# Three tiles for half rows of modulation weights, four for raw weights, and a later point at which a half row is taken

## The chip, the cores and the metric

The kernel runs on one core of a Trainium2 chip. The metric is device time in microseconds for one execution; a difference is judged on several executions of both kernels on the same chip. The core has a matmul engine (TensorE, PE), a vector engine (VectorE, DVE), a scalar engine (ScalarE, ACT), GpSimd (POOL) and SyncE (SP), which issues nearly all DMA transfers of this kernel. Each engine runs its own instructions in program order.

## The reference

A two-layer trunk on 256 tokens of width 2048, in float32. Each layer has a mixer and a SwiGLU FFN; each of the four sub-layers is normalised, modulated and gated by numbers made from one vector `c`:

```python
def ada_modulation(c, w, b):
    mod = (jax.nn.silu(c) @ w + b)[:, None, :]
    shift, scale, gate = jnp.split(mod, 3, axis=-1)
    return shift, scale, gate
...
    shift, scale, gate = ada_modulation(c, ada_mix_w[i], ada_mix_b[i])
    h = rms_norm(x) * (1.0 + scale) + shift
    ...
    x = x + gate * y
```

In layer 0 the mixer is RWKV-7 and a gated delta net side by side behind one input projection and one output projection; in layer 1 it is Mamba-2. The modulation weights are 4 sub-layers × 2048 × 6144 numbers, 201 MB: they are read once and used for one vector only.

## The kernel before

**Weights of the projections.** They come in pieces of up to 128 × 1024 float32 (512 KB), in the order in which they are used (`seq`, made by `plan`). Each is loaded into a *raw* tile (`rawt`, `RAW` of them, line 575). ACT copies it to a reduced-precision high part `whi` (`split_next`, line 697), DVE subtracts to get the low part `wlo` (`low_parts`, line 712), and PE multiplies high by high, high by low and low by high (`products`). A raw tile is free when its low part is made; `issue_raw` (line 594) then has SP load the next piece into it. Of `whi` and `wlo` there are `PARTS` = 3 each.

**Modulation weights.** PE isn't used for them. DVE takes one row of 2048 weights per output channel block: a multiply with silu(c) and a sum. The first 32 rows (shift and scale of the first sub-layer) come whole, 1 MB each, into `INI` = 6 tiles of their own, in `seq` among the first slab's pieces. All other 160 rows come in two halves of 512 KB each, into `adat` tiles (`ADAS` of them, line 587). `adaq` lists the 320 halves in order, each with a due time counted in pieces of `seq`. The functions:

- `issue_ada` (line 617) has SP load the next half into a free `adat` tile, if it is at most `EARLY` = 48 pieces ahead of its due time. While other halves are on the way it waits until the tile's last use lies behind the planned PE clock.
- `take_ada` (line 650) does one half on DVE (`ada_half`), which frees its tile, and calls `issue_ada`.
- `fill_ada` (line 638) decides whether a half is taken now. It is called after each step of `products`, and in `force`.
- `modc` (line 655) is called by whoever needs a shift, scale or gate. If the row isn't known it takes halves until it is, whatever `fill_ada` would say.

**The order of the work.** The program is written in one order by a planner, `Clock`. It keeps an estimated time for each engine (`clock.at`) and for each tile its last write or read (`clock.since`; for a tile that a DMA fills, the estimated landing). In the FFNs and the mixers PE's products set the pace, and everything else is slipped in between by these estimates: `run` steps the chains of the mixer, `prefetch` splits the next piece when DVE and ACT are less than `SOON` = 1000 ns ahead of PE, and `fill_ada` takes halves. Its rule: a half that is due may be taken while DVE's estimate is at most `LATE` = 2000 ns ahead of PE's, one that isn't due only while DVE is at least 500 ns behind (`FILL`).

**The slab.** A sub-layer's first matmuls (`lin_slab`, line 780) run over the 16 input tiles in the outer loop and 14 output tiles (8 in layer 1) inside, so that PE can start when the first input tile is ready. Three tiles ahead, `ahead` makes the input: `norm_mod` multiplies on DVE by the norm, `shifted` (line 838) adds the shift on ACT (`hhi`) and on DVE (`hlo`). The shift comes from `modc`.

**Names in the profile.** `adat` are the half rows (`adap` and `mod` the sums that they give), `ini` the whole rows, `raw` the raw tiles, `whi` and `wlo` the parts, `hhi` and `hlo` the parts of the input, `t` the normed input. All operations are recorded on line 373, where a helper issues them, so groups are told apart by tiles.

Of the kernel before, what the change touches and what calls it, by code (L numbers as in the profile page):

```python
# [85 lines left out]
LAG = 4  # L86
SOON = 1000.0
INI = 6
RAW = 5
PIECE = 8  # L90
LEAD = 2
PARTS = 3
WORK0 = 6
WORK1 = 10
IDLE = 500.0
ADAS = 2
FILL = -500.0
LATE = 2000.0
DUE = 1.0
# [297 lines left out]
def trunk(ctx: ExitStack, tc: tile.TileContext, I, out):  # L397
    nc = tc.nc
    clock = Clock()
# [11 lines left out]
    ET = mybir.EngineType  # L411
# [81 lines left out]
    def force(stop):  # L493

        while not stop():
            c = min((c for c in chains if not blocked(c)), key=lambda c: c.ready)
            fill_ada(c.ready - IDLE)
            step(c)
# [53 lines left out]
    def plan(w, adas):  # L552

        a = [r + (e,) for r in adas for e in range(2)]
        adaq.extend(r + (len(seq) + int(DUE * i * len(w) / len(a)),) for i, r in enumerate(a))
        seq.extend(w)
# [17 lines left out]
    plan(wf1[88:], [])  # L574
    rawt = [wp.tile([P, 1024], F32, name=f"raw{q}") for q in range(RAW)]
    rname = [name_of(t) for t in rawt]
    rfree = list(range(RAW))
    ini = ExitStack()
# [7 lines left out]
    after_ada = {}  # L586
    adat = [wp.tile([P, 1024], F32, name=f"adat{q}") for q in range(ADAS)]
    aname = [name_of(t) for t in adat]
# [28 lines left out]
    def issue_ada():  # L617
        while adaq and len(adas) < ADAS and adaq[0][4] <= st["item"] + EARLY:
            q = next(q for q in range(ADAS) if q not in [a[0] for a in adas])
            if adas and clock.since(aname[q]) > clock.at(ET.PE) + QUEUE:  # L620
                return
            adas.append((q,) + adaq.pop(0))
            load_ada(adat[q], *adas[-1][1:5])
# [14 lines left out]
    def fill_ada(until=None):  # L638

        issue_ada()  # L640
        while adas:
            q, l, r, n, e, due = adas[0]
            v = clock.at(ET.DVE)
            if until is None:
                until = clock.at(ET.PE) + (LATE if due <= st["item"] else FILL)
            if v > until or clock.since(aname[q]) > until:
                return
            take_ada()

    def take_ada():  # L650
        q = adas.pop(0)
        ada_half(adat[q[0]], *q[1:5])
        issue_ada()
# [100 lines left out]
    def products(units, hi, lo, o, act):  # L754

        ahi, alo = act
        n = len(units)
        lag = min(LAG, n)
        w = lambda t, i: t[:, (o + i) * P:(o + i + 1) * P]
        for i in range(n + lag):  # L760
            if i < n:
                ps, kt, a, z = units[i]
                PE.matmul(ps, w(hi, i), ahi[:, kt, :], start=a, stop=False)
                PE.matmul(ps, w(hi, i), alo[:, kt, :], start=False, stop=False)
            if i >= lag:
                ps, kt, a, z = units[i - lag]
                PE.matmul(ps, w(lo, i - lag), ahi[:, kt, :], start=False, stop=z)
            if i % STEP == STEP - 1 or i == n + lag - 1:
                low_parts()
                issue_raw()  # L770
                run()
                if max(clock.at(ET.DVE), clock.at(ET.Activation)) < clock.at(ET.PE) + SOON:
                    prefetch()
                fill_ada()
# [1216 lines left out]
```

## Time and profile before

| | |
|---|---|
| median of 3 runs | 3009.4 us (3009.3 to 3010.23) |
| the profiled execution | 3007.3 us, of which the span of its instructions is 3005.5 us |
| mean granted clock of PE | 0.985 |
| ACT, POOL busy | 1437.3 us, 166.0 us |
| moved by DMA | 706.30 MB, mean 235 GB/s |
| DVE on half rows | 160 × 1322 ns and 160 × 1302 ns |
| half rows: issue to landing | 4.8 us median, 3.2 to 11.6 us |
| raw pieces: issue to landing | 4.2 us median, 2.8 to 11.9 us |

Busy times are unions of an engine's instructions. In a view of waits each row says which instruction stood idle, what ended its wait, then the total in us, the number of times and the longest in us. In a timeline a row has the start in us from the start of the span, the duration in us, and in brackets the idle time before it with what ended it. A view of windows has one row per stretch: busy us of PE, of its weight loads, of DVE, ACT and POOL with their counts, PE's granted clock, the share of the DMA engines and GB/s; restricted to one tile's instructions it has only the engines that these use.

### The profile page before, as it was taken

Reading aid. Unit: us, or ns where it says so; the run is one execution under the profiler, and the core shown is the slowest. Engines: PE = TensorE matmul, PEld = TensorE weight load, DVE = VectorE, ACT = ScalarE, POOL = GpSimd, SP = SyncE. Lnnn points to the kernel's source line nnn. Section 1 sums busy time; section 2 is a strip of 40 time slices with the busy share of each in tenths; the row PEclk is TensorE's granted clock in tenths of the full one; section 3 lists DMA queues with packets and bytes.
Section 4 is the critical chain, followed back from the end, with each engine's and each line's share of the span. In section 5 each row is a group of like instructions: output and inputs, shape, how many; then the busy total and the mean of one; then the engine's idle time right before and its main releaser. Section 6 shows DMA issues by size and latency. Waiting matters only on the chain.

```text
span 3005.5 us, 61406 instructions
## 1 busy us (share of the span) xinstructions
PE 2876.6 (96%) x25098; PEld 2806.8 (93%) x25098; DVE 2198.9 (73%) x3442; ACT 1437.3 (48%) x2363; POOL 166.0 (6%) x191
## 2 busy tenths in 40 slices
PE   6789999997899999999999999999999999999998
PEld 6788889987799999999999999999999999999998
DVE  6987897888777787777778878888767754544555
ACT  3354555544344444444446566555445444444444
POOL 3400001000000000000000111111000000000000
PEclk9899999998999999999999999999999999999999
DMA  9865464576887898788866666666866755655554
GB/s 387 349 199 183 143 216 158 166 276 237 285 285 277 286 331 311 280 284 275 281 208 204 214 208 229 221 225 229 279 221 237 272 184 174 200 184 189 185 174 154
DMA packets 237307, 706.30 MB, mean 235 GB/s; under 512 B 36912, under 2 KB 55648, under 8 KB 236768
## 3 DMA queue, kind: packets, MB, share of 16 engines
q1 hardware_dynamic: 236448, 699.46, 68.4%
q8 instruction: 196, 3.21, 0.4%
q10 hardware_dynamic: 576, 2.92, 0.3%
q14 instruction: 87, 0.71, 0.1%
HBM read 695.70 MB, written 6.58 MB: 234 GB/s over the span
## 4 chain that ended last, share of the span: by engine, by line
issue 52%; PE 21%; DVE 2%; ACT 1%; POOL 0%; DMA 0%; DVEq 0%; POOLq 0%; ACTq 0%
PE bank L373 21%; ACT whi L373 1%; DVE wlo L373 0%; DVE hlo L373 0%; DVE t0b L373 0%; DVE adat L373 0%; DVE x L373 0%; DVE w L373 0%; POOL mgsa L373 0%; DVE ymix L373 0%; DMA adat<-in_ada 0%; DVE mar L373 0%; ACT t L373 0%; DVE mxs L373 0%; DVE sqacc L373 0%
## 5 line engine op out<-in xcount | busy, mean ns | idle before, releaser
L373 PE MATMUL bank<-hhi,whi 128*128 128x256 f32 x5568 | 1472.6, 286 | 38.2 <-ACT whi L373 36.0
L373 PE MATMUL bank<-hlo,whi 128*128 128x256 f32 x5568 | 1450.4, 282 | 3.3 <-DVE hlo L373 2.9
L373 DVE TENSOR_TENSOR wlo<-raw,whi 128x1024 fp32r<-128x1024 f32 (+3 forms) x1005 | 1112.0, 1121 | 422.8 <-ACT whi L373 418.9
L373 ACT ACTIVATE whi<-raw 128x1024 fp32r<-128x1024 f32 (+3 forms) x1005 | 966.5, 971 | 691.5 <-PE bank L373 653.3
L373 PE MATMUL bank<-hhi,wlo 128*128 128x256 f32 x5568 | 1121.8, 284 | 26.2 <-DVE wlo L373 26.0
L373 PEld LDWEIGHTS bank<-hhi,whi 128*128 128x128 f32 x5568 | 1061.0, 191 | 56.5 <-ACT whi L373 42.9
L373 PEld LDWEIGHTS bank<-hlo,whi 128*128 128x128 f32 x5568 | 1061.4, 191 | 6.5 <-DVE hlo L373 4.6
L373 PEld LDWEIGHTS bank<-hhi,wlo 128*128 128x128 f32 x5568 | 858.4, 190 | 37.4 <-DVE wlo L373 31.8
L373 PE MATMUL bank<-glo,whi 128*128 128x256 f32 x1408 | 351.1, 281 | 0.0
L373 PE MATMUL bank<-ghi,whi 128*128 128x256 f32 x1408 | 351.1, 281 | 0.0
L373 PEld LDWEIGHTS bank<-glo,whi 128*128 128x128 f32 x1408 | 265.0, 188 | 0.0
L373 PEld LDWEIGHTS bank<-ghi,whi 128*128 128x128 f32 x1408 | 265.0, 188 | 0.0
L373 PE MATMUL bank<-ghi,wlo 128*128 128x256 f32 x1408 | 229.6, 281 | 0.0
L373 DVE CUSTOM_DVE_ANT_0 adat<-adat,silc,adap 128x1024 f32<-128x1024 f32 x160 | 211.6, 1322 | 22.6 <-DMA adat<-in_ada 22.0
L373 DVE CUSTOM_DVE_ANT_0 adat<-adat,silc,prm 128x1024 f32<-128x1024 f32 x160 | 208.3, 1302 | 13.8 <-DMA adat<-in_ada 13.8
L373 PEld LDWEIGHTS bank<-ghi,wlo 128*128 128x128 f32 x1408 | 193.8, 188 | 0.0
L373 ACT ACTIVATE fs<-bank 128x256 f32<-128x256 f32 x88 | 33.7, 382 | 182.2 <-PE bank L373 182.2
L373 DVE TENSOR_TENSOR fg<-fs,bank 128x256 f32<-128x256 f32 x88 | 37.0, 420 | 113.0 <-ACT fs L373 113.0
L373 DVE SCALAR_TENSOR_TENSOR w<-pad,prm,w 128x256 f32<-128x256 f32 x216 | 110.3, 512 | 5.2
L373 POOL TENSOR_TENSOR rstd<-rpow,half_neg 128x2 f32<-128x2 f32 x5 | 3.5, 697 | 1764.5 <-DVE rpow L373 1764.5
L373 DVE CUSTOM_DVE_ANT_0 ini<-ini,silc,prm 128x2048 f32<-128x2048 f32 x32 | 84.7, 2648 | 17.0 <-ACT tin L373 17.0
L373 DVE SCALAR_TENSOR_TENSOR x<-bank,mod,x 128x256 f32<-128x256 f32 x106 | 50.6, 481 | 45.4 <-PE bank L373 45.4
(254 smaller groups left out, 2028.3 us busy)
## 6 DMA issues: line engine op xcount, KB each, us to landing
raw<-in_ffn SPq DMA_DIRECT2D x324, 512.0 KB, 4.3
adat<-in_ada SPq DMA_DIRECT2D x320, 512.0 KB, 4.8
raw<-in_in SPq DMA_DIRECT2D x238, 512.0 KB, 4.4
raw<-in_ffn SPq DMA_DIRECT2D x128, 384.0 KB, 4.5
raw<-in_ffn SPq DMA_DIRECT2D x128, 320.0 KB, 3.4
raw<-in_out SPq DMA_DIRECT2D x75, 512.0 KB, 4.2
ini<-in_ada SPq DMA_DIRECT2D x32, 1024.0 KB, 11.4
raw<-in_in SPq DMA_DIRECT2D x48, 448.0 KB, 3.9
```

The lines of the kernel that those rows point to most:

```text
L373: r = f(*a, **k)
```

## The change

`RAW` goes from 5 to 4 and `ADAS` from 2 to 3. Both kinds of tiles are 128 × 1024 float32, so the sum is unchanged. In `fill_ada` the second condition is replaced. Before, a half was left when its estimated landing lay behind `until`, that is, later than 2000 ns ahead of PE if it is due (500 ns behind PE if it is not). Now it is left until `LAND` = 1500 ns have passed since the estimated landing, measured on the later of DVE's and PE's estimates. The first condition and `modc` are unchanged.

```diff
-RAW = 5
+RAW = 4
...
-ADAS = 2
+ADAS = 3
+LAND = 1500.0
...
             v = clock.at(ET.DVE)
             if until is None:
                 until = clock.at(ET.PE) + (LATE if due <= st["item"] else FILL)
-            if v > until or clock.since(aname[q]) > until:
+            if v > until or clock.since(aname[q]) + LAND > max(v, clock.at(ET.PE)):
                 return
             take_ada()
```

## The prediction

> **What bounds the kernel now.** I read the page first, then the stage windows, then the waits of single stages, and last the timeline of one repeating piece.
>
> ```profile
> span 3005.5 us, 61406 instructions
> PE 2876.6 (96%) x25098; PEld 2806.8 (93%) x25098; DVE 2198.9 (73%) x3442; ACT 1437.3 (48%) x2363; POOL 166.0 (6%) x191
> ```
>
> TensorE (PE) is busy for 96% of the span, so at most 128.9 us are idle, and the question is where they lie. The windows below cut the span by stage: start-up with the 1 MB modulation rows, the layer-0 mixer, its output projection, the first slab of the first FFN, the rest of that FFN, the layer-1 mixer, the last FFN.
>
> ```profile
> core 0: us, PE busy (x) PEld busy (x) DVE busy (x) ACT busy (x) POOL busy (x), PEclk, DMA share, GB/s
> 0.00:140.00 140.00, 99.16 (x663) 94.72 (x663) 113.69 (x108) 48.87 (x78) 53.80 (x38) 0.94 0.97 385
> 140.00:600.00 460.00, 438.34 (x4666) 401.87 (x4666) 377.35 (x900) 247.15 (x573) 39.42 (x95) 0.97 0.56 177
> 600.00:742.00 142.00, 119.19 (x1057) 111.71 (x1056) 116.40 (x225) 67.04 (x136) 4.14 (x4) 0.95 0.75 270
> 742.00:858.00 116.00, 96.92 (x732) 94.45 (x733) 87.59 (x137) 44.59 (x68) 0.45 (x1) 0.93 0.75 263
> 858.00:1500.00 642.00, 642.00 (x5440) 642.00 (x5441) 484.98 (x662) 281.78 (x364) 0.00 (x0) 1.00 0.83 290
> 1500.00:2400.00 900.00, 886.80 (x7519) 868.38 (x7519) 710.65 (x1051) 487.31 (x806) 67.50 (x53) 1.00 0.68 229
> 2400.00:3005.50 605.50, 594.23 (x5028) 593.70 (x5027) 308.19 (x364) 260.51 (x341) 0.69 (x1) 0.99 0.57 181
> ```
>
> From 858 us on PE is idle for 0 + 13.2 + 11.3 us in 2147.5: nothing that the change can speed up counts there. Idle are 40.8 us in start-up, 21.7 in the mixer, 22.8 in the output projection and 19.1 in the slab. In the slab the granted clock is 0.93 as well, while no engine and no DMA engine is full (DVE 87.6 of 116 us, DMA share 0.75). The stage is bound by a latency. Its waits, first PE's and then DVE's:
>
> ```profile
> PE bank L373 <- ACT whi L373: 17.4, 8, 3.4
> PE bank L373 <- DVE wlo L373: 1.2, 1, 1.2
> PE bank L373 <- POOL rstd L373: 1.0, 1, 1.0
> ```
>
> ```profile
> DVE wlo L373 <- ACT whi L373: 12.4, 13, 1.0
> DVE adat L373 <- DMA adat<-in_ada: 9.5, 11, 1.2
> ```
>
> PE waits for whi, which ACT makes in less time than PE uses it, so ACT must be held by something else. The timeline of one inner tile shows the whole chain:
>
> ```profile
> 760.86 1.28 DVE L373 CUSTOM_DVE_ANT_0 adat<-adat,silc,prm 128x1024 f32<-128x1024 f32 x1
> ...
> 762.18 0.33 SPq L373 DMA_DIRECT2D adat<-in_ada  x1
> ...
> 763.51 0.33 SPq L373 DMA_DIRECT2D adat<-in_ada  x1
> ...
> 767.73 1.28 DVE L373 CUSTOM_DVE_ANT_0 adat<-adat,silc,prm 128x1024 f32<-128x1024 f32 x1 [0.40 <-DMA adat<-in_ada]
> ...
> 770.22 1.28 DVE L373 CUSTOM_DVE_ANT_0 adat<-adat,silc,adap 128x1024 f32<-128x1024 f32 x1 [1.20 <-DMA adat<-in_ada]
> ...
> 771.89 0.51 ACT L373 ACTIVATE hhi<-t,mod 128x256 fp32r<-128x256 f32 x1 [5.84 <-DVE t L373]
> 772.30 1.77 ACT L373 ACTIVATE whi<-raw 128x896 fp32r<-128x896 f32 x2
> ...
> 773.29 0.39 PE L373 MATMUL bank<-hhi,whi 128*128 128x256 f32 x1 [2.83 <-ACT whi L373]
> ```
>
> Two half rows are taken at 760.86 and right after it. Each take frees its tile, and only then SyncE (SP) issues the next half: at 762.18 and 763.51. They land at 767.73 and 770.22, where DVE has stood waiting, so 5.55 and 6.71 us after the issue. The second gives the shift that ACT's hhi needs; ACT stands 5.84 us in front of it, and the weights' whi is behind hhi in ACT's order. PE then stands for 2.83 us. Two tiles allow one pair per (landing + take), about 7 us, and PE follows.
>
> **The change part by part.** Durations are those of the profiled execution, which took 3007.3 us for its span of 3005.5; the median of the three runs is 3009.4, so 2.1 us are added to carry a sum over to it. A difference under 0.2% (6 us) counts as no change.
>
> *Third half-row tile and the later take, in the slab.* The tile's DMA is issued one take earlier in the ring: three halves in the air instead of two. The time of three is still one landing and one take, 6.71 + 1.28 = 8.0 us, so a pair every 5.3 us is possible instead of every 7. The LAND rule then keeps DVE from being queued at a half that has not landed; only the forced takes in modc ignore it. Of the 9.5 us that DVE waits here I take all as gone. PE gets them back about one for one: in the quoted tile 1.60 us of landing waits stand before a PE wait of 2.83. That is −9.5, of at most 19.6 us that PE waits for in this stage. What is late next is DVE itself: wlo and the takes.
>
> ```profile
> 140.00:600.00 460.00, 55.48 (x44) 0.97 0.56 177
> 600.00:742.00 142.00, 41.30 (x33) 0.95 0.75 270
> 742.00:858.00 116.00, 37.19 (x29) 0.93 0.75 263
> ```
>
> These rows count the takes: 44, 33 and 29, at 1.28 us of DVE each. The takes needed by the end of the slab's shifts are the first 96, so of the slab's 29 nineteen or so are forced by it and the rest are merely due. In bursts before the slab a third tile allows one take more each time; I put three fewer takes into the slab's path, −3.0 with their read-out, between 0 and −13 (10 × 1.28). The landing rule also lets the ten that are only due pass by until they have landed.
>
> The clock: PE is granted 0.93 in 116 us, which is 8.1 us of a full clock; I take −3.0 of it, from 0 to −8.
>
> ```profile
> 784.00:792.00 8.00, 4.90 (x30) 4.70 (x29) 6.00 (x9) 2.19 (x3) 0.00 (x0) 0.81 0.74 254
> 800.00:808.00 8.00, 5.96 (x37) 5.96 (x38) 6.32 (x12) 3.17 (x5) 0.00 (x0) 0.79 0.74 266
> ```
>
> In these two stretches of the slab the clock falls to 0.81 and 0.79, with PE idle for 3.1 and 2.0 us in each. [...]
>
> Slab: −9.5 − 3.0 − 3.0 = −15.5.
>
> *The same in the output projection (600 to 742).*
>
> ```profile
> DVE adat L373 <- DMA adat<-in_ada: 14.5, 14, 2.8
> ```
>
> ```profile
> PE bank L373 <- ACT whi L373: 7.7, 4, 5.3
> PE bank L373 <- DVE Big L373: 5.5, 1, 5.5
> PE bank L373 <- DVE sqacc L373: 4.6, 1, 4.6
> PE bank L373 <- DVE hlo L373: 2.6, 2, 1.9
> ```
>
> DVE waits 14.5 us for landings. But halves are behind their due times here, so freed DVE time turns into takes that come earlier (14.5 / 1.28 is eleven of them), which is what empties the slab. PE's own waits are on single late DVE steps (Big, sqacc, hlo: 12.7 us), which an earlier landing may help and one more take in front may worsen. I take −2, between −12.7 and +4 (three more takes in front of such steps).
>
> *Mixer (140 to 600).* PE is idle for 21.7 us here, and more takes per burst compete with the chains for DVE. I take +1, between −4 and +4 (three takes fewer or more in front of the chains' steps).
>
> *Start-up.* A third half row of 512 KB is issued among the 1 MB rows.
>
> ```profile
> 50.00:100.00 50.00, 38.57 (x288) 37.13 (x287) 49.79 (x47) 19.71 (x28) 27.16 (x14) 0.93 1.02 407
> ```
>
> DVE is busy for 49.79 of 50 us and sets the pace; the DMA queue runs beside it at 407 GB/s with stock to spare, as DVE never waits for a row. The extra half costs 524 KB / 407 GB/s = 1.3 us of queue, hidden by that stock: 0, at most +1.3. One raw tile less only delays an issue into a queue that is still full: 0.
>
> *Four raw tiles.* A raw tile is issued when the lo part of its old content is done, and SP stands there nearly always:
>
> ```profile
> SPq L373 <- DVE wlo L373: 1638.6, 860, 10.6
> ```
>
> ```profile
> 1000.00:1100.00 100.00, 43.61 (x48) 39.57 (x48) 1.00 0.89 307
> ```
>
> ```profile
> DMA to landing us min/median/max: 4.0/5.2/5.9
> ```
>
> These two rows are of the raw tiles alone in the narrowest stage, 1000 to 1100 us: a piece every 100 / 48 = 2.08 us, DVE 0.91 and ACT 0.82 us for one, landing 5.2 us after the issue. Four tiles give a round trip of 4 × 2.08 = 8.3 us, of which 5.2 + 0.82 + 0.91 = 6.9 are needed: 1.4 us to spare, where five leave 3.5. Behind that PE has up to two finished pieces as cover. Queued behind a late raw issue on SP are the half rows and the next raws. I take +1.5 for all stages, between 0 and +6, a third of what the starving rival below costs.
>
> **Sum.** −15.5 − 2 + 1 + 0 + 1.5 = −15.0: 3007.3 − 15.0 = 2992.3 for the profiled execution, 2994.4 for the median. Half of the way to every bound at once would give about 2978 to 3005; the terms do not all go one way, so I take two thirds of that, 2984 to 3001, as this case's own range.
>
> **The rivals.**
>
> *DVE takes the landing's place.* In the quoted tile a pair of takes, wlo and the two mod steps already fill most of 7 us, and DVE also waits 12.4 us for whi. If all 29 takes stay in the slab, freed waits come back as DVE waiting for whi, and about half of the 9.5 us is won: −5, with nothing elsewhere, 3004. For it: DVE is at 76% in the stage and the hhi, whi, wlo chain is serial. Against: ten of the 29 takes are not needed there.
>
> *The catch-up is complete.* All shifts are known ahead of the slab, PE never stands there: −19.6 − 8.1, and −5 of the 12.7 before it: −32.7, 2977. For it: three tiles in the air nearly always. Against: DVE is busy for 116.4 of 142 us before the slab.
>
> *Raw tiles starve (slower).* Three halves in the air put 524 KB more ahead of a raw piece: at the 385 GB/s of start-up 1.36 us of landing. Added to 6.9 that is 8.3, exactly the round trip of four tiles; from there each further us costs a quarter of it per piece, and PE's two pieces of cover run dry. With 0.5 us over, on 48 pieces and as many in the like stages (about 144 in all): 144 × 0.5 / 4 = 18 us, less the slab's 9.5: +8.5, 3018. For it: DMA share 0.89 and a landing of up to 5.9 us in that stage. Against: takes there go by their due times, so three halves are seldom in the air at once.
>
> *The rule only refuses.* The stricter LAND leaves halves until modc forces them, with the same wait as now: the time stays at 3009. It is counted with the first rival.
>
> **How the numbers follow.** Forecast 0.47 (2994); DVE in its place, with the refusing rule, 0.18 (3004 to 3009); complete catch-up 0.17 (2977); starving 0.18 (3018). Faster by over 0.2% (under 3003.4) hold the forecast and the catch-up: 0.64. Within 0.2%: 0.18. Slower: 0.18. The range for 8 in 10 goes from 2980, which leaves out about half of the catch-up, to 3013, which leaves out the upper half of the starving.
>
> **What would show it.** Right: DVE's wait for the landing of adat falls from 9.5 us in the slab to under 2; PE's wait for whi there from 17.4 to under 6; the slab's stretch gets shorter by about 15 us with a clock over 0.97; takes before the slab rise above 77. RAW right: no waits of whi on a raw landing beyond a few us, and PE still at 642 of 642 in the long FFN stretch. Wrong: DVE stands in the slab on whi instead, or PE idles after 858 us with whi waiting on raw landings, or the number of takes in the slab stays at 29 and its length with it.

## The result and the profile after

The changed kernel takes 2988.2 us (median of 6 runs, 2984.91 to 2990.38) against 3009.82 us for the kernel before in the same sessions (6 runs, 3006.53 to 3012.51). The medians differ by 21.6 us, where 15.0 were forecast; the ratio is 0.9924, with a 95% interval of 0.9914 to 0.9934. The profiled execution took 2988.43 us for a span of 2986.6, and its span is 18.9 us below the one before; the comparison of the two traces can explain only these 18.9.

The page's head and the stage windows of the kernel after:

```profile
span 2986.6 us, 61337 instructions
PE 2873.8 (96%) x25098; PEld 2805.3 (94%) x25098; DVE 2196.8 (74%) x3442; ACT 1438.3 (48%) x2363; POOL 163.3 (5%) x191
```

```profile
core 0: us, PE busy (x) PEld busy (x) DVE busy (x) ACT busy (x) POOL busy (x), PEclk, DMA share, GB/s
0.00:140.00 140.00, 98.97 (x663) 94.62 (x663) 114.36 (x109) 49.86 (x78) 53.85 (x38) 0.94 0.97 385
140.00:600.00 460.00, 433.11 (x4631) 397.54 (x4633) 382.13 (x905) 246.59 (x573) 40.89 (x94) 0.97 0.57 183
600.00:742.00 142.00, 127.38 (x1107) 119.45 (x1108) 122.00 (x240) 69.56 (x142) 5.20 (x5) 0.94 0.79 279
742.00:858.00 116.00, 110.86 (x904) 109.85 (x904) 94.47 (x140) 53.20 (x76) 0.00 (x0) 0.96 0.83 290
858.00:1500.00 642.00, 641.77 (x5433) 641.57 (x5431) 481.87 (x662) 281.18 (x366) 0.00 (x0) 1.00 0.85 288
```

PE's idle time falls from 3005.5 − 2876.6 = 128.9 to 2986.6 − 2873.8 = 112.8 us, that is by 16.1 of the 18.9. In the window 742 to 858 PE does 904 matmuls in place of 732. Windows at fixed times no longer cover the same work, though, so the slab is measured below by its own marks: from the last product of PE for the norm in front of it (rstd) to the first step of ACT behind it. The first fence is the kernel before, the second the kernel after; in each, the first row is of all engines and the second of the takes alone (DVE busy with their count, granted clock, DMA share, GB/s).

```profile
743.30:848.10 104.80, 89.68 (x679) 87.41 (x678) 81.97 (x122) 38.47 (x53) 0.00 (x0) 0.93 0.78 271
743.30:848.10 104.80, 37.19 (x29) 0.93 0.78 271
```

```profile
738.10:823.70 85.60, 83.91 (x678) 82.47 (x677) 73.35 (x110) 38.76 (x52) 0.00 (x0) 0.97 0.86 301
738.10:823.70 85.60, 29.34 (x23) 0.97 0.86 301
```

The same products take 85.6 us in place of 104.8, and 23 half rows are taken among them in place of 29. PE stands idle for 85.60 − 83.91 = 1.7 us, where it was 15.1. The waits that bore the forecast, in the windows used there, are these: DVE's wait in the output projection, then over the whole run, then PE's wait in the slab.

```profile
DVE adat L374 <- DMA adat<-in_ada: 0.4, 1, 0.4
```

```profile
DVE adat L374 <- DMA adat<-in_ada: 1.3, 2, 0.8
```

```profile
PE bank L374 <- ACT whi L374: 5.1, 3, 3.5
```

In the slab DVE has no landing wait left (9.5 us before); in the output projection 14.5 us became 0.4, over the whole run 35.8 became 1.3; PE's wait for whi falls from 17.4 to 5.1. The timeline of an inner tile of the slab shows takes without waits:

```profile
759.50 1.28 DVE L374 CUSTOM_DVE_ANT_0 adat<-adat,silc,adap 128x1024 f32<-128x1024 f32 x1
...
764.56 1.28 DVE L374 CUSTOM_DVE_ANT_0 adat<-adat,silc,prm 128x1024 f32<-128x1024 f32 x1
765.88 1.28 DVE L374 CUSTOM_DVE_ANT_0 adat<-adat,silc,adap 128x1024 f32<-128x1024 f32 x1
...
767.54 0.51 ACT L374 ACTIVATE hhi<-t,mod 128x256 fp32r<-128x256 f32 x1 [4.19 <-DVE t L374]
```

The second take of a pair starts as soon as the first ends, 1.32 us after the start of the first. hhi starts 0.4 us after the second take ends, as before; only the landing in front of the takes is gone.

**Where the 18.9 us arose.** Both kernels split the same weight pieces in the same order, so the moment at which ACT begins the split of a given piece can be compared between the two traces. The differences (after minus before, worked out from the two traces):

```
piece                                   before at      after - before
32   start-up's slab done               149.4 us            -1.3
122  end of the mixer's input           596.5 us            +2.4
165  first piece of the FFN's slab      729.6 us            -4.3
197  slab done                          843.2 us           -24.3
280  in the rest of the first FFN      1063.4 us           -21.3
520  layer 1's mixer begins            1660.1 us           -21.4
665  near its end                      2127.9 us           -19.9
745  last FFN                          2362.9 us           -18.9
1004 last piece                        2987.2 us           -18.9
```

So start-up gives −1.3, the mixer +3.7, the output projection −6.7, the slab −20.0, and the rest +5.4: 3.0 right behind the slab, −0.1 in the rest of that FFN, +1.5 in layer 1's mixer, +1.0 behind it. In the stretch right behind the slab PE is busy nearly throughout in both kernels (54.62 of 54.80 us before, 56.33 of 56.50 after), and takes are caught up: 13 in 56.5 us where 10 stood in 54.8. The fences are the takes of this stretch, before and after.

```profile
857.60:912.40 54.80, 12.64 (x10) 0.97 0.82 285
```

```profile
833.30:889.80 56.50, 16.62 (x13) 0.95 0.84 295
```

### The profile page after: what moved, and what is told of

Same layout as the page of the kernel before. It is cut to its first block, busy times and chain, and to the rows that moved or that the text cites. A ratio compares the mean times of both kernels' runs of the same rounds, so it can differ in the third digit from the quotient of the medians.

```text
span 2986.6 us, 61337 instructions
## 1 busy us (share of the span) xinstructions
PE 2873.8 (96%) x25098; PEld 2805.3 (94%) x25098; DVE 2196.8 (74%) x3442; ACT 1438.3 (48%) x2363; POOL 163.3 (5%) x191
## 4 chain that ended last, share of the span: by engine, by line
PE 41%; issue 26%; DVE 3%; ACT 2%; POOL 0%; DMA 0%; DVEq 0%; POOLq 0%; ACTq 0%
PE bank L374 41%; DVE wlo L374 1%; ACT whi L374 1%; ACT mar L374 1%; DVE w L374 0%; DVE ymix L374 0%; DVE t0b L374 0%; DVE adat L374 0%; DMA raw<-in_in 0%; DVE x L374 0%; POOL mgsa L374 0%; DVE mxs L374 0%; DVE mar L374 0%; ACT w L374 0%; ACT pad L374 0%
## 5 line engine op out<-in xcount | busy, mean ns | idle before, releaser
L374 DVE CUSTOM_DVE_ANT_0 adat<-adat,silc,adap 128x1024 f32<-128x1024 f32 x160 | 204.6, 1279 | 1.5 <-DMA adat<-in_ada 0.8
```

Of the source, the lines that this page charges most:

```text
L374: r = f(*a, **k)
```

## The experiments

All kernels below compute the full reference. Each is named by what it has: the number of raw tiles, of half-row tiles, and which rule. The slab is always measured by the marks above.

**The three parts alone, and the margin.** Three kernels do one part each; the fourth takes only the margin out of the change.

*raw_alone*: four raw tiles, two half-row tiles, the old rule.

```diff
-RAW = 5
+RAW = 4
```

> Four raw tiles alone; two half-row tiles and the old rule. Theory (the third half-row tile and the later take make the gain, four raw tiles cost little): 1 to 4 us slower than before, 3011 to 3014, with ACT waiting about 30 us more for raw landings and PE hardly. Rival (raw tiles starve): 8 to 18 us slower. Second rival (fewer raw tiles hold the weight loads back and so help the half rows): faster than before.

*tiles_alone*: four raw tiles and three half-row tiles, the old rule. (No run has five raw tiles with three half-row tiles; the change keeps the sum of both kinds at seven.)

```diff
-RAW = 5
+RAW = 4
...
-ADAS = 2
+ADAS = 3
```

> Four raw and three half-row tiles with the old rule. Theory: the ring of two tiles was the limit in the first slab of the first FFN, so the third tile alone brings most: 8 to 16 us faster than before (2994 to 3002), the slab's 116 us stretch shorter by 8 or more, some DVE waits for half-row landings left (5 to 15 us in all). Rival (the rule makes the gain, the tile only serves it): within 4 us of before, DVE waits for half-row landings still over 25 us.

*rule_alone*: five raw tiles, two half-row tiles, the new rule.

```diff
+LAND = 1500.0
...
-            if v > until or clock.since(aname[q]) > until:
+            if v > until or clock.since(aname[q]) + LAND > max(v, clock.at(ET.PE)):
```

> Five raw and two half-row tiles with the new rule. Theory: with two tiles the later take makes the ring slower, more halves are left to be forced by the code that needs the shift: 0 to 10 us slower than before (3010 to 3020), DVE waits for landings in the slab stay at 6 us or more. Rival (the rule makes the gain): 12 to 22 us faster, 2988 to 2998.

*land_0*: the kernel after, without the margin.

```diff
-LAND = 1500.0
+LAND = 0.0
```

> The changed kernel with LAND = 0: a half is taken as soon as its estimated landing is reached on the later of DVE's and PE's estimates. Theory: real landings come later than the estimate (4.8 us median against 3.7 planned), so DVE waits again for landings, 5 to 15 us in all, a third of it reaches PE: 2 to 6 us slower than the changed kernel (2990 to 2995). Rival (the margin is idle, only the comparison with the later estimate counts): within 1 us of the changed kernel.

Measured, with the slab from each profile:

```
kernel        median of runs          ratio to before, 95%      slab  takes  landing waits  PE's wait for whi
raw_alone     3000.63 (8 runs)    0.9963 [0.9949, 0.9977]    87.1   23       3.1            3.1
tiles_alone   2991.71 (5)         0.9932 [0.9918, 0.9946]    86.2   23       0.6            2.4
rule_alone    2990.27 (6)         0.9928 [0.9912, 0.9945]    90.8   23       1.7            5.9
land_0        2986.43 (6)         0.9922 [0.9904, 0.9939]    84.6   22       0              1.9
```

The third tile, with four raw tiles, gave nearly the whole change: 19.2 us by the medians, more than the 8 to 16 expected. The rest did not go by the theory. The new rule alone, expected slower by 0 to 10 us, gained about as much. Four raw tiles alone, expected 1 to 4 us slower, gained 0.4%, though its profiled execution was the fastest of its eight (2990.92 us; up to 3005.33), so its slab may flatter it. Its second rival had expected it faster, because fewer weight loads would let the half rows land sooner; over the whole run they do not, their median from issue to landing being 5.0 us there against 4.8. Nor is the slab all of it: by the comparison of pieces raw_alone and rule_alone are 9.0 and 14.1 us ahead of before when the slab begins and 24.2 and 30.4 when it is done, and lose 7.8 and 9.5 by the end. And the margin is worth nothing that these runs can tell, as the rival for land_0 had it: the intervals of land_0 and of the kernel after overlap. Over the whole run DVE waits for landings in land_0 as much as this, which costs it nothing:

```profile
DVE adat L374 <- DMA adat<-in_ada: 15.0, 24, 2.3
```

Three edits that have little in common, each with half of the gain or more, asked for something that they share. It is in the counts: of the 96 half rows that must be taken by the end of the slab, the kernel before has taken 74 when the slab's first piece is split, the kernel after 81, and the three parts alone 80, 81 and 77. Before falls behind in the mixer: from 311 to 373 us it takes none at all, and it has taken 44 at 600 us, where the kernel after has 49. The gain could thus be a head start alone (fewer takes left for the slab), with the landing waits following from it, or the third tile's latency, or both. The second batch separates them.

**Head start and latency apart.**

*before_due085*: the kernel before, with due times 15% earlier: a head start, two tiles, the old rule.

```diff
-DUE = 1.0
+DUE = 0.85
```

> The kernel before, with DUE = 0.85 in place of 1.0 and nothing else: due times come earlier, so that in the written order 81 half rows are taken ahead of the first slab of the first FFN instead of 75; two half-row tiles, five raw tiles and the old rule stay. Theory now (the slab's length is set by how many of the 96 needed half rows are still to be taken in it): 10 to 22 us faster than before, 2988 to 3000, the slab shorter by 12 or more. Rival (the third tile or the rule is what counts, and the other kernels gained for reasons of their own): within 4 us of before.

*after_held*: the kernel after, with eight half rows of the first FFN's gate, not needed in the slab, queued ahead of its scales and shifts: three tiles without the head start.

```diff
-    plan(w0 + pieces("out0"), ada_of(0, (2,)) + ada_of(1, (1, 0))[:-late])
+    plan(w0 + pieces("out0"), ada_of(0, (2,)) + ada_of(1, (2,))[:4] + ada_of(1, (1, 0))[:-late])
...
-    plan(wf0[own:], ada_of(1, (2,)) + ada_of(2, (1, 0, 2)))
+    plan(wf0[own:], ada_of(1, (2,))[4:] + ada_of(2, (1, 0, 2)))
```

> The changed kernel with four gate rows of the first FFN (8 half rows) put into the queue ahead of its scales and shifts: only 76 of the 96 half rows that the slab needs are taken ahead of it, as before. Theory of the head start alone: the slab is 8 to 16 us longer than in the changed kernel, 2996 to 3006. Theory that three tiles lift the latency limit (a pair every 5.3 us instead of 7): the slab is longer by 0 to 5 us, 2986 to 2994.

*two_tiles_land_due09*: rule_alone with due times 10% earlier, which in its written order left it behind at the slab (69 taken).

```diff
-DUE = 1.0
+DUE = 0.9
```

> Five raw and two half-row tiles, the new rule, DUE = 0.9: by the written order only 70 half rows are taken ahead of the slab (77 with DUE = 1.0). Head start and ring of two: 26 are left, a pair takes 7 to 8 us, so the slab gets 10 to 20 us longer than with DUE = 1.0: 3000 to 3012. Rival (the rule makes the gain, whatever the head start): 2986 to 2995.

*two_tiles_raw4_land*: four raw tiles and the new rule, two half-row tiles: the change without its third tile.

```diff
-ADAS = 3
+ADAS = 2
```

> Four raw and two half-row tiles with the new rule: 72 half rows are taken ahead of the slab by the written order. Head start and ring of two: 8 to 18 us slower than five raw tiles with the same rule (which took 77), 2998 to 3010, nearly all of it in the slab. Rival (the rule makes the gain): 2986 to 2995, plus up to 4 for waits on raw landings.

Measured ("needed" are the takes that count towards the 96 and lie before the split of the slab's first piece):

```
kernel                 median           ratio to before, 95%     needed  slab   takes  landing waits  PE's wait for whi
before                                                             74    104.8   29       9.5           13.9
after                                   0.9924 [0.9914, 0.9934]    81     85.6   23       0              1.7
before_due085          3009.23 (12)     0.9994 [0.9982, 1.0006]    80     97.5   24       6.1           10.6
after_held             3000.4  (12)     0.9968 [0.9957, 0.998]     74     95.4   30       0              9.5
two_tiles_land_due09   3014.4  (12)     1.0013 [1.0001, 1.0024]    69    112.6   30      12.9           21.0
two_tiles_raw4_land    3021.28 (7)      1.0037 [1.0022, 1.0052]    72    108.1   28       9.8           15.7
```

The rows of the slab in after_held, first of the takes and then of all engines, and the landing waits of DVE in the slab of two_tiles_raw4_land and of two_tiles_land_due09:

```profile
741.70:837.10 95.40, 37.98 (x30) 0.96 0.88 307
741.70:837.10 95.40, 85.91 (x678) 84.04 (x677) 82.17 (x124) 38.45 (x52) 0.00 (x0) 0.96 0.88 307
```

```profile
DVE adat L374 <- DMA adat<-in_ada: 9.8, 9, 1.7
```

```profile
DVE adat L374 <- DMA adat<-in_ada: 12.9, 9, 2.7
```

Two costs come apart. With three tiles and seven takes more, after_held has no landing wait at all, and its slab is 95.4 − 85.6 = 9.8 us longer: 1.40 us for a take, about its 1.28 us on DVE and the step to the next. With as many takes and two tiles there are 9.5 to 12.9 us of landing waits, and they come on top: before's slab is 104.8 − 95.4 = 9.4 us longer than after_held's, with one take fewer and 9.5 us of landing waits. So take 85.6 us, 1.40 for each take over 23 and 1.1 for each us of landing wait. The kernels after, after_held and before gave these three numbers, so they are no test of them. The others are: 109.6 and 103.4 come out for the two kernels with two tiles and the rule (measured 112.6 and 108.1), 93.7 for before_due085 (97.5) and 87.5 for rule_alone (90.8). These four come out 3 to 5 us too short, and raw_alone 1.9 too long (89.0 against 87.1): the prices hold within 5 us, not better. The theory that the landing is the whole of it falls: it expected after_held's slab 0 to 5 us longer. The one of a head start alone gave 8 to 16 us for that kernel, and 9.8 is inside; but it expected before_due085 10 to 22 us faster, and that kernel's time did not move and its slab is longer by 12 than after's. The rule by itself falls too: with two tiles and no head start it saves nothing, and both such kernels are no faster than before (3014.4 and 3021.28 us are above even the 3000 to 3012 and 2998 to 3010 expected). two_tiles_land_due09 differs from rule_alone by its due times alone, and these made another order of it: 69 taken in place of 77, and a slab of 112.6 in place of 90.8. What rule_alone won hangs on that order.

before_due085 shows one thing more: its slab is 7.3 us shorter, and its time the same. In its profile it enters the slab 4.0 us later (747.3 against 743.3 us) and loses 4.3 between pieces 520 and 665, in layer 1's mixer; that execution, 3016.65 us, is 7.4 above the kernel's median.

**The floor of the slab, and raw tiles.**

*raw_3*: the kernel after with one raw tile less, for the threshold that the prediction had worked out for starving.

```diff
-RAW = 4
+RAW = 3
```

> The changed kernel with three raw tiles in place of four. Round trip of three tiles in the narrowest stage: 3 x 2.08 = 6.2 us against 6.9 needed, so PE should starve there: 0.23 us for each of some 144 narrow pieces is 30 us or more, 3010 to 3060, PE no longer busy for all of the long FFN stretch. Rival (the landing and PE's finished pieces cover it still): 2986 to 3000.

*slab_spared*: the kernel after, with the rest of the half rows planned behind the slab, so that none but the needed ones are taken in it. *before_spared*: the same edit on the kernel before.

```diff
-    plan(wf0[own:], ada_of(1, (2,)) + ada_of(2, (1, 0, 2)))
+    plan(wf0[own:2 * KT], [])
+    plan(wf0[2 * KT:], ada_of(1, (2,)) + ada_of(2, (1, 0, 2)))
```

> The changed kernel with the gate rows of the first FFN falling due only after the slab's 32 pieces: by the written order 20 half rows are taken in the slab instead of 23. Theory (each take in the slab costs its 1.36 us of DVE, as the held-back kernel showed with 9.8 us for seven): up to 4 us shorter, limited by the 1.7 us that PE still idles there and its clock of 0.97: 2983 to 2987. Rival (the slab has reached PE's own pace): 2986 to 2990.

> The kernel before with the gate rows of the first FFN falling due only after the slab's 32 pieces; two half-row tiles, five raw tiles, the old rule: by the written order 25 half rows in the slab instead of 29, and those that are only due no longer make DVE wait there. Theory: 4 x 1.36 us and 2 to 4 us of landing waits less in the slab, 5 to 10 us faster than before: 3000 to 3006. Rival (only a third tile helps the slab): within 3 us of before.

Measured:

```
kernel          median          ratio to before, 95%      slab   takes  landing waits  PE's wait for whi
raw_3           3059.21 (4)     1.0159 [1.0138, 1.0179]    96.4   23       0             6.3
slab_spared     2983.04 (5)     0.991  [0.9896, 0.9924]    85.1   20       0             1.7
before_spared   3012.41 (11)    1.0004 [0.9994, 1.0014]    98.2   25       5.9          12.8
```

The waits of ACT for raw pieces over the whole run, first in the kernel after, then in raw_3 (total us, times, longest):

```profile
ACT whi L374 <- DMA raw<-in_in: 21.6, 19, 4.3
...
ACT whi L374 <- DMA raw<-in_out: 10.2, 7, 3.2
ACT whi L374 <- DMA raw<-in_ffn: 10.0, 7, 2.7
```

```profile
ACT whi L374 <- DMA raw<-in_ffn: 302.9, 193, 6.2
ACT whi L374 <- DMA raw<-in_in: 128.4, 67, 6.7
...
ACT whi L374 <- DMA raw<-in_out: 45.6, 25, 5.4
```

Four raw tiles make 41.8 us of such waits, three 476.9, and the kernel with three is 71 us above the one with four, just inside the 3010 to 3060 expected. (Its marks of the slab take in 716 matmuls, not 678; between pieces 165 and 197 its slab is 4.3 us longer than the kernel after's, not 10.8.) The stretch that never stood before, 858 to 1500 us, shows it in raw_3:

```profile
858.00:1500.00 642.00, 626.61 (x5230) 620.97 (x5230) 439.24 (x597) 268.22 (x347) 0.00 (x0) 1.00 0.78 268
```

PE is idle there for 15.4 us and does 5230 matmuls where the kernel after does 5433. So the working of the starving rival was right in kind: a piece every 2.08 us gives three tiles a round trip of 6.2 us where 6.9 are needed, and four one of 8.3. The threshold lies between three and four tiles. The size of the shortfall isn't confirmed: in raw_3 itself, from 1000 to 1100 us, the landing takes 4.4 us in the median and up to 6.4, not 5.2, so that by this sum three tiles fall short at the later landings and not at each. In raw_3's last FFN pieces 745 to 1004, where only 15 of the 320 half rows still move, cost nothing: the delay against before is 53.7 us at their start and 52.3 at their end.

slab_spared has three takes fewer than the kernel after and its slab is 0.5 us shorter, not 4.2: below some 23 takes PE's own pace ends the stage (PE idles 1.7 us in it with 23 and with 20). Its time lies in the 2983 to 2987 expected, but not by the shorter slab that was the reason given. before_spared was expected 5 to 10 us faster and isn't: it wins 6.6 us in the slab by four takes and 3.6 us of landing waits, is 5.2 us ahead of before at piece 197, and gives it back: 4.0 up to piece 520 and 6.1 in layer 1's mixer, between pieces 520 and 665. slab_spared is the fastest version seen; its interval overlaps that of the change.

Layer 1's mixer sorts the kernels. Between pieces 520 and 665 each differs from before by this much (raw_3, which starves, left out):

```
three half-row tiles   after +1.5   tiles_alone +0.3   land_0 +0.3   slab_spared +0.5   after_held +1.4
two half-row tiles     rule_alone +3.1   before_due085 +4.3   before_spared +6.1   raw_alone +9.2
                       two_tiles_land_due09 +14.0   two_tiles_raw4_land +16.1
```

Half rows of the last FFN move there, with chains of the mixer beside them. With three tiles no written order loses over 1.5 us; with two tiles every edit of the order lost 3 to 16, with four raw tiles as with five. The kernel before, at 0, is the best of the two-tile orders there. Which chain the takes collide with, no run singled out. Each number is of one profiled execution; those of before_due085 and two_tiles_land_due09 took 7 and 9 us more than their kernels' medians, and raw_alone's 10 us less, so these three are rough.

## Why the prediction was right

The case forecast came about: faster, by the slab. The measured 2988.2 us lie inside the range, 2980 to 3013; the gain was 6.6 us larger than forecast, or 3.9 by the profiled executions. That it came so near is in part luck: by the pieces the slab, the output projection and the start-up won 4.5, 4.7 and 1.3 us more than forecast, while the mixer and the rest of the run lost 2.7 and 3.9 us more.

**The landing waits of the slab** (−9.5, got back one for one): they went, as forecast. DVE has none left, PE's wait for whi fell by 12.2 in the same marks (13.9 to 1.7), and between after_held and before, with nearly equal takes, 9.5 us of such waits are worth 9.4 + 1.4 = 10.8 us of slab. Not all of this is time in which PE stands: of the 9.4, PE's idle time makes up 5.6 (15.1 to 9.5), and for the other 3.8 PE is busy longer with the same products.

**Fewer takes in the slab** (three, −3.0): a mis-sized term. Six went, and a take left in the slab costs 1.40 us by after_held, so this term is −8.4 by that price. The bound of −13 held it. The step that was off is the one from the output projection: the prediction had counted that the 14.5 us freed there hold eleven takes, "which is what empties the slab", and then took three for the slab. The rows of the takes in the mixer and in the output projection of the kernel after, to be held against 44 and 33 before:

```profile
140.00:600.00 460.00, 62.27 (x49) 0.97 0.57 183
600.00:742.00 142.00, 43.50 (x35) 0.94 0.79 279
```

Up to 742 us 84 are taken in place of 77, so the sign came true ("above 77"). But five of the seven were gained in the mixer, and two in the output projection, where the freed time mostly made the stage itself shorter. That a third tile allows more takes in the bursts before the slab is borne out; that the waits freed in the output projection empty the slab is not.

**The clock** (−3.0): 7% of 104.8 us is 7.3 us of a full clock, 3% of 85.6 is 2.6, so 4.7 came back. The sign is right, and the clock ended at the 0.97 that was to be exceeded. PE's busy time says the same: 89.68 us before and 83.91 after for the same products, 5.8 us. These 5.8 are contained in the prices of 10.8 for the landings and 8.4 for the takes, which therefore leave nothing of the 19.2 for a clock term beside them. Split by what PE does, seven takes more in after_held are 7.8 us of PE's idle time, 1.1 for each; in the prediction's own terms the slab's −19.2 is then about −6.7 for the landings, −6.7 for the six takes and −5.8 for the clock. The first was forecast too large and the other two too small. This split rests on one profiled execution of each of the three kernels. PE's waits for whi by the slab's marks, before and after:

```profile
PE bank L373 <- ACT whi L373: 13.9, 7, 3.1
```

```profile
PE bank L374 <- ACT whi L374: 1.7, 2, 1.2
```

Finer windows show where the clock goes. In the kernel before, the slab has four stretches at half clock. The first, with 4.8 us in the slab at a clock of 0.50, sets in at 737.8 us, within a wait of PE of 4.6 us that ends at 740.4, in front of the slab. The other three, each behind the window of 3.41 us that comes before it, are in the last six rows below. The three begin at 789.00, 802.65 and 823.13 us, so 4 and 6 times 3.41 us apart. The first two rows lie on the same steps and share PE's wait of 2.83 us, the one in front of the matmul at 773.29.

```profile
768.52:771.93 3.41, 1.93 (x17) 1.73 (x15) 2.21 (x6) 0.04 (x1) 0.00 (x0) 1.00 0.88 306
771.93:775.35 3.42, 2.06 (x17) 2.06 (x18) 2.40 (x4) 2.14 (x3) 0.00 (x0) 1.00 0.79 295
785.59:789.00 3.41, 0.99 (x8) 0.99 (x9) 2.39 (x5) 2.19 (x3) 0.00 (x0) 1.00 0.97 386
789.00:792.41 3.41, 3.41 (x18) 3.41 (x18) 3.37 (x5) 0.00 (x0) 0.00 (x0) 0.51 0.56 154
799.24:802.65 3.41, 1.06 (x9) 0.86 (x9) 2.39 (x5) 2.01 (x3) 0.00 (x0) 1.00 0.99 378
802.65:806.07 3.42, 3.42 (x19) 3.42 (x18) 3.38 (x5) 0.18 (x1) 0.00 (x0) 0.51 0.53 182
819.72:823.13 3.41, 0.72 (x8) 0.52 (x6) 2.06 (x5) 1.41 (x3) 0.00 (x0) 1.00 0.88 296
823.13:826.55 3.42, 3.42 (x16) 3.42 (x17) 3.36 (x5) 1.17 (x2) 0.00 (x0) 0.51 0.76 260
```

Each of the three times the half clock (0.51) lasts 3.41 us. Waits of 3.10, 2.35 and 2.69 us that leave PE busy for 0.72 to 1.06 us of the window ahead of it come before these. The wait of 2.83 us is divided over the two windows of the first rows, with 1.93 and 2.06 us of busy PE, and the clock stays full (1.00). So in these four cases the length of the gap alone doesn't decide, as 2.35 us came before a half clock and 2.83 didn't; PE's busy time in the window, at most 1.06 us against at least 1.93, tells the four apart. The kernel after keeps in its slab only the stretch behind the wait in front of it:

```profile
738.10:743.40 5.30, 5.30 (x20) 4.67 (x19) 4.14 (x10) 3.15 (x6) 0.00 (x0) 0.50 0.00 0
743.40:823.70 80.30, 78.61 (x660) 77.81 (x659) 69.21 (x101) 35.62 (x46) 0.00 (x0) 1.00 0.92 321
```

In front of this first stretch PE waits 4.6 us in the kernel before and 4.1 in the kernel after; the other three stretches of the kernel before come behind waits of 2.35 to 3.10 us. No run changed the gaps alone, or PE's work around them, so what sets the clock isn't shown.

**The output projection** (−2): −6.7 by the pieces, within its bounds but more than three times the forecast. PE's longest single wait there, 5.5 us on Big, is not among its waits after, and whi fell from 7.7 to 4.6:

```profile
PE bank L374 <- ACT whi L374: 4.6, 3, 3.5
PE bank L374 <- DVE sqacc L374: 4.1, 1, 4.1
```

**The mixer** (+1): +3.7, just inside its +4, with five takes more in it. **Start-up** (0): −1.3. **Four raw tiles** (+1.5 for all stages): the rest of the run lost 5.4, and waits of whi on raw landings rose from 10.2 us to 41.8, more than the "few us" that were the sign; PE is busy for 641.77 us of the long FFN stretch's 642, as the other sign had it. The prediction also read SP as standing "nearly always" at wlo; its 1638.6 us are 55% of the span. How much of the 5.4 is theirs stays open. 3.0 came right behind the slab, with three takes more in the stretch, and 1.5 in layer 1's mixer, where the five kernels with four raw and three half-row tiles lose 0.3 to 1.5. The price of the fifth raw tile by itself, with three half-row tiles, was not measured.

**The rivals.** "DVE takes the landing's place" did not decide here but is real: after_held is that kernel, at 95.4 us of slab without any landing wait and 3000.4 us in all. The complete catch-up, 2977, was not reached; its condition, all shifts known ahead of the slab, was met by no kernel (at most 81 of the 96 were taken by then). Starving begins one tile lower. "The rule only refuses" isn't what rule_alone showed: it won 0.7% on five raw tiles. In the two other kernels with the rule and two half-row tiles nothing was won. What the prediction lacked was this: the parts do not add up. Of the 0.8%, raw_alone has 0.4, and tiles_alone (with its four raw tiles) and rule_alone have 0.7 each. Each also rewrites the order in which the work is issued, as the counts of takes ahead of the slab show, and the kernel before had a poor one for the slab.

## What to carry to other kernels

By the sum used here, which is an estimate, a ring of buffers keeps up when the period of one item is longer than (landing + use) / (number of buffers). For the raw tiles that was 2.08 us against 6.9 / 3 = 2.3 with three, which starved (476.9 us of ACT's waits for raw pieces), and against 6.9 / 4 = 1.7 with four, which hardly did (41.8 us; 6.9 with the landing of the kernel before). Where a planner writes the order, count how many items are already done as the critical stage begins before putting a gain down to latency. A third half-row tile left the slab free of landing waits even where the order came late (0 us in after_held, 9.5 in the kernel before), while the good order of rule_alone, with two, lost its gain at the next small edit. The parts of a change need runs of their own: here four raw tiles with the third half-row tile gave 0.7%, the rule 0.7%, and all together 0.8%.

## What was not expected of the hardware

Waits in a trace can cost nothing: land_0 has 15.0 us of landing waits of DVE, the kernel after 1.3, and their times can't be told apart. A slab that is 7 us shorter can also be worth nothing at the end: before_due085 and before_spared gave it back, much of it some 1000 us later in another layer, so a stage's gain has to be followed to the end of the run. And a busy PE is not always PE at its pace. The full rows of the stretch behind the slab, before and after:

```profile
857.60:912.40 54.80, 54.62 (x454) 54.63 (x455) 40.02 (x51) 24.64 (x32) 0.00 (x0) 0.97 0.82 285
```

```profile
833.30:889.80 56.50, 56.33 (x454) 56.34 (x455) 43.92 (x57) 24.63 (x32) 0.00 (x0) 0.95 0.84 295
```

The same 454 matmuls take 1.7 us longer with PE busy for all but 0.2 us in both; the granted clock, 0.95 against 0.97, makes up about 1.1 of it (0.02 of 56.5, rounded as the clock is). Both stretches begin at the end of a wait of PE of 3.45 us (at 857.77 and 833.47 us); the half clock (0.50) that sets in within it lasts 3.4 us in the kernel before (857.3 to 860.7 us) and 6.8 in the kernel after (832.1 to 838.9).
